# Unread matmuls ahead of the first rows and at the first norm's broadcast, rows loaded ahead of weights, and the sample's first states loaded ahead of stores

## The chip, the cores and the metric

The kernel runs on one core of one Trainium2 chip. The metric is the device time of one execution in microseconds, the median of several runs. The engines are TensorE (PE; its weight loads are listed as PEld), VectorE (DVE), ScalarE (ACT), GpSimd (POOL) and SyncE (SP), which here only issues DMAs.

## The reference

One step of a decoder layer is computed for 1024 prompt rows and 32 sample rows (8 batches of 4), width 1024, in float32:

```python
def hybrid_layer(x, lp, ssd_conv_prev, ssm_prev, ffn_conv_prev, kv_buf):
    hn = rmsnorm(x, lp['norm1'])
    z, xbc, dt_raw, q, k, v = jnp.split(hn @ lp['w_in'], SPLITS, axis=-1)
    y_ssd, ssd_conv_new, ssm_new = ssd_mixer(z, xbc, dt_raw, ssd_conv_prev, ssm_prev, lp)
    ...   # q and k are normed; the window of attention is 128
    x = x + jnp.concatenate([y_ssd, y_att], axis=-1) @ lp['w_out']
    hn = rmsnorm(x, lp['norm2'])
    u, ffn_conv_new = causal_dwconv(hn @ lp['w_up'], ffn_conv_prev, lp['ffn_conv_w'], lp['ffn_conv_b'])
    gate, val = jnp.split(u, 2, axis=-1)
    x = x + (jax.nn.silu(gate) * val) @ lp['w_down']
    return x, (ssm_new, ssd_conv_new, k_new, v_new, ffn_conv_new)
```

The SSD mixer convolves x, B and C over four rows, scans chunks of 128 rows with a carried state for 8 heads, multiplies by silu(z) and norms. For the sample the scan starts from given states (`h0`); for the prompt from zero. All new states are outputs.

## The kernel before

The 1056 rows of prompt and sample are the columns of `xT`; the width of 1024 is eight tiles of 128 partitions, `x[0]` to `x[7]`. Products in float32 are done as three matmuls: each operand is split into a high part (`xh`, `uh`, by ScalarE) and a low part (`xl`, `ul`, by VectorE), and high by high, high by low and low by high are added up. `dense` (L147) does this over three column parts of 352, `token_major` (L199) with rows of 128 tokens.

**Start.** `ones` is a 128x128 tile of ones (L207). For each k the rows `x[k]` are loaded (L222; k = 0 in three parts) and split, their squares are summed into `ssum`, and for even k 256 columns of the two first weights `w01` are loaded (L115). All loads are issued by SP, in the order of the code. The norm is applied late: the matmuls run on rows that are not yet normed, `stats` (L155) sums the squares over partitions with `ones`, VectorE computes `rstd` (L134 to L140), and `bcast` transposes it with the identity (L170) and ScalarE copies it to `rstd_bc` (L171), by which `conv_in` multiplies the matmuls' results (L261). Ahead of `bcast` stands the first `token_major` product, `kv0`.

**Middle.** A string `PLAN` lists units of work: SSD chunks (u), z blocks, splits, output pieces (o). In `ssd_unit` the state step is a matmul into `st` (L660) followed by VectorE's `sn` (L668). For the sample the unit loads the states of the past in four pairs (`h0`, in two buffers; L682), multiplies with them (L685), and stores the rows of this step to `smps` (L678, L679).

**Second norm and FFN.** The rows are held in halves of 528 columns (tp = 0, 1) as `acc`. `out_piece(m, q)` adds the output projection (L778). `half_prep(tp)` calls `half_rstd(tp)`, which sums squares (L852), computes `v` on VectorE (L854, then L134 to L140), transposes it (L859) and copies it (ACT, L861); then eight products by the norm (L871) and the splits into `x2h` (ACT L883) and `x2l` (DVE L884, with differences L888) follow. The up projection is seven products per pair of tiles and half (`product`, L990), its operands made from the weights by L923, L925, L935 and L936, its results combined by L998, L1004, L1010, L1012 and others. Then come the convolution, the gate and the down projection (L1105).

A scheduler of the framework orders each engine's instructions by its own timeline, so that the order on an engine is not that of the code, and an edit early in the program can move rows much later.

Of the kernel before, what the change touches and what calls it, by code (L numbers as in the profile page):

```python
# [9 lines left out]
F32 = mybir.dt.float32  # L10
F32R = mybir.dt.float32r
I32 = mybir.dt.int32
AF = mybir.ActivationFunctionType
# [5 lines left out]
T = 1056  # L19
NP = 1024  # L20
NS = 32
NB = 8
NPAIR = 22
EPS = 1e-6
NEG = -1e30
PC = 352
# [20 lines left out]
def kernel(ctx, tc, xT, wxbc, wkv, wq, wz, wout, wup, wdn, cols, rows, cst, idm,  # L47
# [61 lines left out]
    def unit():  # L109
        return (wr.tile([128, 1024], F32, tag="raw", name="raw"), wp.tile([128, 1024], F32R, tag="uh", name="uh"),  # L110
                wp.tile([128, 1024], F32R, tag="ul", name="ul"))

    def load_part(u, src, a, b, e=None):
        raw, hi, lo = (t[:, a:b] for t in u)
        sp.dma_start(out=raw, in_=src)  # L115
        act.activation(out=hi, in_=raw, func=AF.Copy)  # L116
        n = (b - a) // (1 if e else 1)
        for i in range(0, b - a, n):
            (e or dve).tensor_tensor(out=lo[:, i:i + n], in0=raw[:, i:i + n], in1=hi[:, i:i + n].bitcast(F32),  # L119
                                     op=ALU.subtract)  # L120
# [41 lines left out]

    def bcast(pp):

        for a, n in ((0, 512), (512, 512), (NP, NS)):
            ps = bank(pp)
            for o in range(0, n, 128):
                m = min(n, 128)
                t = (a + o) // 128
                pe.transpose(out=ps[:, o:o + m], in_=b3(rstd[:m, t:t + 1], m, 128), identity=ident[:m, :m])  # L170
            act.activation(out=rstd_bc[:, a:a + n], in_=ps[:, :n], func=AF.Copy)  # L171
# [33 lines left out]


    dve.memset(ones, 1.0)  # L207
    act.activation(out=rstd[:, 0:1], in_=ones[:, 0:1], func=AF.Exp)
    x = [None] * 8
    with tc.tile_pool(name="st", bufs=1, side="right", reuse_waits="tile") as stp:  # L210
        ssum = stp.tile([128, T], F32, name="ssum")
        w01 = [unit(), unit()]
        for k in range(8):
            if k % 2 == 0:
                for m in range(2):
                    load_part(w01[m], wxbc[m][:, 128 * k:128 * k + 256], 128 * k, 128 * k + 256)
            if k == 0:
                sp.dma_start(out=colt, in_=cols)
            xr = yp.tile([128, T], F32, tag="y", name="xr")
            x[k] = x_pair(xp)  # L220
            for a, b in ([(0, PC), (PC, 2 * PC), (2 * PC, T)] if k == 0 else [(0, T)]):
                sp.dma_start(out=xr[:, a:b], in_=xT[k][:, a:b])  # L222
                split(xr[:, a:b], x[k], col(C_N1 + k), a, b)
            if k == 0:
                act.activation(out=ssum, in_=xr, func=AF.Square)
            else:
                sq = stp.tile([128, T], F32, tag="sq", name="sq", bufs=2)
                act.activation(out=sq, in_=xr, func=AF.Square)
                dve.tensor_tensor(out=ssum, in0=ssum, in1=sq, op=ALU.add)
        w01 = [u[1:] for u in w01]  # L230
        sp.dma_start(out=idt, in_=idm)
        wkvu = [load_unit(wkv[:, 3 * i:min(8, 3 * i + 3), :].rearrange("p k c -> p (k c)"), 264 * min(3, 8 - 3 * i))
                for i in range(3)]
        sp.dma_start(out=sstt, in_=sst)
        sp.dma_start(out=rowt, in_=rows)
        sp.dma_start(out=cs, in_=cst[:, 0:K_LOW])
        dve.tensor_scalar(out=chalf, in0=colt[:, C_CW:C_CW + 40], scalar1=0.5, scalar2=None, op0=ALU.mult)
        two = pc.tile([128, 2, 512], F32, tag="sc", name="two")
        ps01 = [[bank(pm) for _ in range(3)], [two[:, 0], two[:, 1], bank(pq)]]
        for k in range(8):  # L240
            for m in range(2):
                for p in range(3):
                    dense(ps01[m][p][:, :PC], wl(w01[m]), xr_(x, p), [k], first=k == 0, last=k == 7)
                if k == 7 and m == 0:
                    stats(stp, ssum, pq)
        kv0 = token_major(264, wkvu, 3, 0, bank(pq))
        bcast(pq)
# [350 lines left out]
    def ssd_unit(g, t, p, carry, te):  # L598
# [5 lines left out]
        hs = slice(4 * g, 4 * g + 4)  # L604
        px = psd.tile([128, 512], F32, tag="px", name="px", bufs=2)
        if smp:
            f4 = p.tile([128, 512], F32, tag="Cs", name="f4", bufs=2)[:, 0:384].rearrange("p (i c t) -> p i c t", i=3, c=4)
            for i, f in enumerate((x0, x1, Bm)):
                pool.tensor_copy(out=f4[:, i], in_=b3(f[:, tok].unsqueeze(1), 128, 4, NS))
# [65 lines left out]
                      rhs=xw[:m, 64 * h:64 * h + 64], start=True, stop=True)  # L675
        cm = p.tile([128, 8, NS], F32, tag="cm", name="cm", bufs=1)
        pool.tensor_tensor(out=cm, in0=b3(Cm[:, NP:T].unsqueeze(1), 128, 8, NS), in1=bmask, op=ALU.mult)
        sp.dma_start(out=smps[g, :, 0:128], in_=bt)  # L678
        sp.dma_start(out=smps[g, :, 128:384], in_=xd)  # L679
        for j in range(4):  # L680
            h0 = p.tile([128, 2, 256], F32, tag="h0", name="h0", bufs=2)
            sp.dma_start(out=h0, in_=h0T[:, g, 2 * j:2 * j + 2])  # L682
            for b in range(2):
                r = slice(32 * (2 * j % 4 + b), 32 * (2 * j % 4 + b) + 32)
                pe.matmul(out=yy[r, 256:512], lhsT=cm[:, 2 * j + b], rhs=h0[:, b], start=j < 2, stop=j >= 2)  # L685
        y = p.tile([128, 256], F32, tag="xd0", name="ys")
        dve.tensor_tensor(out=h4(y), in0=h4(yy[:, 256:512]),
                          in1=b3(te[:, 8 + 4 * g:12 + 4 * g].unsqueeze(2), 128, 4, 64), op=ALU.mult)
# [160 lines left out]
    def half_rstd(tp):  # L849
        ps = bank()  # L850
        for j in range(6):
            pe.matmul(out=ps[:88, j:j + 1], lhsT=ssum[tp][:, 88 * j:88 * j + 88], rhs=ones[:, 0:1], start=True, stop=True)  # L852
        v = pt_.tile([128, 2, 6], F32, tag="v2", name="v2")
        dve.tensor_scalar(out=v[:88, 0], in0=ps[:88, 0:6], scalar1=1.0 / D, scalar2=EPS, op0=ALU.mult, op1=ALU.add)  # L854
        rsqrt(pt_, v[:88, 1], v[:88, 0], 88, 6)
        for q in range(2):
            ps = bank()
            for j in range(3):
                pe.transpose(out=ps[:, 88 * j:88 * j + 88], in_=b3(v[:88, 1, 3 * q + j:3 * q + j + 1], 88, 128),  # L859
                             identity=ident[:88, :88])  # L860
            act.activation(out=ssum[tp][:, q * QC:q * QC + QC], in_=ps[:, :QC], func=AF.Copy)  # L861
        return ssum[tp]

    X2 = [{}, {}]

    def half_prep(tp):

        rb = half_rstd(tp)
        for m in (4, 5, 6, 7, 0, 1, 2, 3):
            h = half(m, tp)  # L870
            dve.scalar_tensor_tensor(out=h, in0=h, scalar=col(C_N2 + m), in1=rb, op0=ALU.mult, op1=ALU.mult)  # L871
# [73 lines left out]
    for i, m in enumerate((4, 5, 6, 7, 0, 1, 2, 3)):  # L945
        if i >= 4:
            w[m] = None
        for q in (2, 3):
            out_piece(m, q)
            if i == 0 and q == 2:  # L950
                half_prep(0)
        half_done(m, 1, i == 0)
    up_load(0)
    for j in range(7):
# [93 lines left out]
    for n, (cp, groups) in enumerate(SETS):  # L1048
        for g in groups:
# [15 lines left out]
                conv(cp, 0)  # L1065
            last = (n, *g), done
            if g == (0, 0):
                half_prep(1)
    product(*last[0], 6)
    conv(last[0][1], 1)  # L1070
    sp.dma_start(out=fco, in_=fcot)
# [188 lines left out]
```

## Time and profile before

| | us |
|---|---|
| median of three runs | 1192.26 |
| the three runs | 1192.59, 1192.26, 1187.1 |
| the profiled execution | 1191.26 |
| its span | 1189.5 |
| TensorE busy in it | 1149.4 (97%) |
| VectorE busy in it | 906.0 (76%) |
| ScalarE busy in it | 513.0 (43%) |

The mean granted clock of TensorE over the span is 0.990. The profile shows one execution; an engine's share is a mean over stages, so that each stage has to be looked at by itself. In rows of the profile an engine is followed by the line of the kernel, the operation and `output<-inputs`; text in brackets is the idle time ahead and what ended it.

### The profile page before, as it was taken

What the parts mean: (1) busy time and instruction counts of PE and PEld (TensorE: products, weight loads), DVE (VectorE), ACT (ScalarE), POOL (GpSimd) and SP (SyncE); (2) the same over time, 40 slices, a digit from 0 to 9 for tenths busy, and PEclk for the clock granted to TensorE, in tenths of its full rate; (3) what the DMA queues carried; (4) which work ended last, traced back from release to release, by engine and by line L of the source; (5) the groups of instructions that cost most, each with busy time, mean ns of one, the idle gap of its engine ahead of it and who ended that gap; (6) DMA issues with size and microseconds to landing.
All of it is one profiled execution on the core that took longest, in us unless ns stands there. A gap on an engine that the chain in (4) does not pass through costs nothing.

```text
span 1189.5 us, 22050 instructions
## 1 busy us (share of the span) xinstructions
PE 1149.4 (97%) x8614; PEld 1106.5 (93%) x8614; DVE 906.0 (76%) x1886; ACT 513.0 (43%) x1048; POOL 134.8 (11%) x300
## 2 busy tenths in 40 slices
PE   8899989999979999899999999999999999999998
PEld 7899878888957999789999999999999999999998
DVE  7678868666888578998777777787777877677764
ACT  7435553446774334555455454545454421112110
POOL 0000001022253000011011010101010011001000
PEclk9999989998999999899999999999999999999999
DMA  8111102113465523122222222222222944224203
GB/s 295 63 60 62 33 19 75 48 50 111 131 221 160 173 73 131 36 81 98 74 72 90 73 90 73 90 73 81 81 71 75 380 149 160 97 91 133 92 9 147
DMA packets 52360, 122.52 MB, mean 103 GB/s; under 512 B 9232, under 2 KB 19984, under 8 KB 52240
## 3 DMA queue, kind: packets, MB, share of 16 engines
q1 hardware_dynamic: 52256, 121.12, 29.8%
q8 instruction: 67, 1.10, 0.4%
q14 instruction: 37, 0.30, 0.1%
HBM read 94.86 MB, written 27.26 MB: 103 GB/s over the span
## 4 chain that ended last, share of the span: by engine, by line
PE 89%; DVE 7%; DMA 2%; ACT 1%; issue 1%; SPq 0%; POOL 0%; DVEq 0%; ACTq 0%
PE ps L147 40%; PE ps L990 35%; PE ps L199 7%; PE sc L503 1%; PE ps L525 1%; DVE x2l L884 1%; DVE au L936 1%; DVE c L1032 1%; PE two L147 1%; DMA raw<-in_wup 1%; PE ps L517 1%; PE yy L653 1%; PE st L660 1%; PE ps L339 0%; PE px L611 0%
## 5 line engine op out<-in xcount | busy, mean ns | idle before, releaser
L990 PE MATMUL ps<-x2h,au 128*128 128x264 f32 x2464 | 456.1, 286 | 8.5 <-DVE au L936 2.8
L990 PEld LDWEIGHTS ps<-x2h,au 128*128 128x128 f32 x2464 | 385.0, 189 | 10.6 <-DVE au L936 3.5
L990 PE MATMUL ps<-x2l,au 128*128 128x264 f32 x1232 | 349.4, 285 | 0.1
L990 PEld LDWEIGHTS ps<-x2l,au 128*128 128x128 f32 x1232 | 232.8, 189 | 0.3 <-DVE x2l L884 0.3
L1105 DVE TENSOR_TENSOR acc<-acc,ps 128x352 f32<-128x352 f32 x264 | 131.5, 517 | 66.0 <-PE ps L147 65.5
L147 PE MATMUL ps<-xh,uh 128*128 128x264 f32 (+3 forms) x528 | 163.3, 315 | 8.9 <-ACT xh L182 5.9
L147 PE MATMUL ps<-gh,ul 128*128 128x352 f32 x528 | 170.1, 322 | 0.0
L147 PE MATMUL ps<-gl,uh 128*128 128x352 f32 x528 | 170.0, 322 | 0.0
L147 PE MATMUL ps<-gh,uh 128*128 128x352 f32 x528 | 167.8, 322 | 0.0
L147 PE MATMUL ps<-xh,ul 128*128 128x264 f32 (+3 forms) x528 | 163.7, 311 | 0.0
L147 PE MATMUL ps<-xl,uh 128*128 128x264 f32 (+3 forms) x528 | 163.3, 310 | 0.3 <-POOL xl L180 0.3
L116 ACT ACTIVATE uh<-raw 128x1024 fp32r<-128x1024 f32 (+3 forms) x59 | 55.9, 953 | 188.0 <-PE ps L147 166.9
L1032 DVE SCALAR_TENSOR_TENSOR c<-u,colt,c 128x1072 f32<-128x1072 f32 x88 | 116.7, 1329 | 3.6 <-ACT c L1030 3.6
L147 PEld LDWEIGHTS ps<-xh,uh 128*128 128x128 f32 x528 | 99.7, 190 | 13.7 <-ACT xh L182 6.3
L147 PEld LDWEIGHTS ps<-xl,uh 128*128 128x128 f32 x528 | 100.6, 191 | 1.8 <-POOL xl L180 0.9
L147 PEld LDWEIGHTS ps<-xh,ul 128*128 128x128 f32 x528 | 100.6, 190 | 1.0 <-issue 0.3
L936 DVE TENSOR_TENSOR au<-raw,au 128x512 fp32r<-128x512 f32 x115 | 78.8, 690 | 27.3 <-ACT au L935 27.3
L147 PEld LDWEIGHTS ps<-gl,uh 128*128 128x128 f32 x528 | 99.2, 188 | 0.4
L147 PEld LDWEIGHTS ps<-gh,ul 128*128 128x128 f32 x528 | 99.3, 188 | 0.0
L147 PEld LDWEIGHTS ps<-gh,uh 128*128 128x128 f32 x528 | 98.8, 188 | 0.0
L935 ACT ACTIVATE au<-raw 128x512 fp32r<-128x512 f32 x115 | 71.0, 625 | 60.7 <-DVE raw L923 31.5
L119 DVE TENSOR_TENSOR ul<-raw,uh 128x1024 fp32r<-128x1024 f32 (+3 forms) x55 | 60.5, 1105 | 7.0 <-ACT uh L116 6.9
(290 smaller groups left out, 1768.4 us busy)
## 6 DMA issues: line engine op xcount, KB each, us to landing
raw<-in_wup SPq DMA_DIRECT2D x46, 512.0 KB, 3.5
gr<-gd SPq DMA_DIRECT2D x22, 528.0 KB, 5.3
gd<-c SPq DMA_DIRECT2D x22, 512.0 KB, 2.6
raw<-in_wdn SPq DMA_DIRECT2D x22, 512.0 KB, 3.8
raw<-in_wout SPq DMA_DIRECT2D x12, 512.0 KB, 3.4
acc<-in_xT SPq DMA_DIRECT2D x16, 264.0 KB, 5.0
accd<-acc SPq DMA_DIRECT2D x16, 264.0 KB, 2.5
acc<-accd SPq DMA_DIRECT2D x8, 528.0 KB, 8.4
```

Of the source, the lines that this page charges most:

```text
L116: act.activation(out=hi, in_=raw, func=AF.Copy)
L119: (e or dve).tensor_tensor(out=lo[:, i:i + n], in0=raw[:, i:i + n], in1=hi[:, i:i + n].bitcast(F32), op=ALU.subtract)
L147: pe.matmul(out=ps, lhsT=w(a, k), rhs=x(b, k), start=first and k == ks[0] and i == 0, stop=last and k == ks[-1] and i == 2)
L199: pe.matmul(out=ps[:m, :n], lhsT=x[k][c][:, a:a + m], rhs=w[k // nk][b][:, o:o + n], start=k == 0 and i == 0, stop=k == 7 and i == 2)
L503: pe.matmul(out=sb[:, v, c].rearrange("p i k -> p (i k)"), lhsT=qT[a][r, c], rhs=kT[b][r, o:o + 256], start=i == 0, stop=i == 2)
L517: pe.transpose(out=pt[:, h], in_=P[:, h], identity=ident)
L525: pe.matmul(out=po[64 * v:64 * v + 64, 0:256].rearrange("p (c q) -> p c q", c=2), lhsT=(vall[:, t - i] if i or not t else vdif[:, t - 1])[ ...
L935: act.activation(out=u[:, 0:512], in_=src, func=AF.Copy)
L936: dve.tensor_tensor(out=u[:, 512:1024], in0=src, in1=u[:, 0:512].bitcast(F32), op=ALU.subtract)
L990: pe.matmul(out=ps, lhsT=wgt[:, 512 * a + 128 * k:512 * a + 128 * k + 128], rhs=xx[b][:, k], start=opens and k == 0 and i == 0, stop=k == ...
L1032: dve.scalar_tensor_tensor(out=c[:, 0:n], in0=u[:, j:j + n], scalar=col(C_FW + 3 * m + j), in1=c[:, 0:n], op0=ALU.mult, op1=ALU.add)
L1105: dve.tensor_tensor(out=o, in0=o, in1=ps[:, :PC], op=ALU.add)
```

## The change

It has five parts.

1. Ahead of everything else on TensorE stand nine matmuls of `ones` by `ones` (`NWARM`), whose result nobody reads.
2. The first 352 columns of `x[0]` are the first load on SP, then the constants `colt`; the first two weight parts are issued on ScalarE's queue, ahead of its first activation, which brings the table load. For k = 2, 4, 6 nothing moves between queues.
3. `bcast` begins with ten unread matmuls of `ones` into a bank of its own.
4. In the sample's SSD unit the first two pairs of states are loaded at the start of the unit, and the stores to `smps` stand behind the loop over the states.
5. `half_prep` is cut in two: for the first half the sum of squares and `v` come after the output piece (4, 2) as before, and the transposes and the rest after the piece (4, 3). For the second half both stay together.

```diff
+NWARM = 9
...
     def load_part(u, src, a, b, e=None):
         raw, hi, lo = (t[:, a:b] for t in u)
-        sp.dma_start(out=raw, in_=src)
+        if src is not None:
+            sp.dma_start(out=raw, in_=src)
...
     def bcast(pp):
 
+        hold = bank(pp)
+        for i in range(10):
+            pe.matmul(out=hold[:, 0:128], lhsT=ones, rhs=ones, start=True, stop=True)
...
     dve.memset(ones, 1.0)
-    act.activation(out=rstd[:, 0:1], in_=ones[:, 0:1], func=AF.Exp)
     x = [None] * 8
+
+    idle = bank(pq)
+    for i in range(NWARM):
+        pe.matmul(out=idle[:, 0:128], lhsT=ones, rhs=ones, start=True, stop=True)
     with tc.tile_pool(name="st", bufs=1, side="right", reuse_waits="tile") as stp:
         ssum = stp.tile([128, T], F32, name="ssum")
         w01 = [unit(), unit()]
+        for m in range(2):
+            act.dma_start(out=w01[m][0][:, 0:256], in_=wxbc[m][:, 0:256])
+        act.activation(out=rstd[:, 0:1], in_=ones[:, 0:1], func=AF.Exp)
         for k in range(8):
-            if k % 2 == 0:
+            xr = yp.tile([128, T], F32, tag="y", name="xr")
+            x[k] = x_pair(xp)
+            if k == 0:
+                sp.dma_start(out=xr[:, 0:PC], in_=xT[k][:, 0:PC])
+                sp.dma_start(out=colt, in_=cols)
+                for m in range(2):
+                    load_part(w01[m], None, 0, 256)
+            elif k % 2 == 0:
                 for m in range(2):
                     load_part(w01[m], wxbc[m][:, 128 * k:128 * k + 256], 128 * k, 128 * k + 256)
-            if k == 0:
-                sp.dma_start(out=colt, in_=cols)
-            xr = yp.tile([128, T], F32, tag="y", name="xr")
-            x[k] = x_pair(xp)
             for a, b in ([(0, PC), (PC, 2 * PC), (2 * PC, T)] if k == 0 else [(0, T)]):
-                sp.dma_start(out=xr[:, a:b], in_=xT[k][:, a:b])
+                if k or a:
+                    sp.dma_start(out=xr[:, a:b], in_=xT[k][:, a:b])
                 split(xr[:, a:b], x[k], col(C_N1 + k), a, b)
...
         if smp:
+
+            h0s = []
+            for j in range(2):
+                h0s.append(p.tile([128, 2, 256], F32, tag="h0", name="h0", bufs=2))
+                sp.dma_start(out=h0s[j], in_=h0T[:, g, 2 * j:2 * j + 2])
...
-        sp.dma_start(out=smps[g, :, 0:128], in_=bt)
-        sp.dma_start(out=smps[g, :, 128:384], in_=xd)
         for j in range(4):
-            h0 = p.tile([128, 2, 256], F32, tag="h0", name="h0", bufs=2)
-            sp.dma_start(out=h0, in_=h0T[:, g, 2 * j:2 * j + 2])
+            if j < 2:
+                h0 = h0s[j]
+            else:
+                h0 = p.tile([128, 2, 256], F32, tag="h0", name="h0", bufs=2)
+                sp.dma_start(out=h0, in_=h0T[:, g, 2 * j:2 * j + 2])
...
+        sp.dma_start(out=smps[g, :, 0:128], in_=bt)
+        sp.dma_start(out=smps[g, :, 128:384], in_=xd)
...
+        return v
+
+    def half_bcast(tp, v):
...
-    def half_prep(tp):
-
-        rb = half_rstd(tp)
+    def half_prep(tp, v):
+
+        rb = half_bcast(tp, v)
...
             if i == 0 and q == 2:
-                half_prep(0)
+                v0 = half_rstd(0)
+            elif i == 0:
+                half_prep(0, v0)
...
             if g == (0, 0):
-                half_prep(1)
+                half_prep(1, half_rstd(1))
```

Lines move with the edit: L147 becomes L149, L170 becomes L175, L199 becomes L204, L682 becomes L626 (first two pairs) and L703, L774 becomes L797, L871 becomes L897, L884 becomes L910, L936 becomes L962, L998 becomes L1026 and L1012 becomes L1040.

Three places show what this makes of the engines' orders. The first is TensorE at the broadcast. Before, the last rows of `kv0` (L199) are followed by the transposes of `rstd` (L170):

```order
L199 MATMUL ps<-uh,xh 128x264
L199 MATMUL ps<-uh,xl 128x264
L199 MATMUL ps<-ul,xh 128x264
L170 MATMUL ps<-idt,rstd 128x128 x8
L170 MATMUL ps<-idt,rstd 128x32
```

After, at the same place, with L204 for `kv0`, L169 for the unread matmuls and L175 for the transposes:

```order
L204 MATMUL ps<-ul,xh 128x264
L169 MATMUL ps<-ones 128x128 x4
L204 MATMUL ps<-uh,xh 128x264
L204 MATMUL ps<-uh,xl 128x264
L169 MATMUL ps<-ones 128x128 x2
L204 MATMUL ps<-ul,xh 128x264
L204 MATMUL ps<-uh,xh 128x264
L204 MATMUL ps<-uh,xl 128x264
L204 MATMUL ps<-ul,xh 128x264
L169 MATMUL ps<-ones 128x128 x4
L175 MATMUL ps<-idt,rstd 128x128 x8
L175 MATMUL ps<-idt,rstd 128x32
```

The ten unread matmuls stand among the last six of `kv0`, four of them right ahead of the transposes.

The second place is SP's queue at group 0's second pair and group 1's first pair of states (`h`). Before:

```order
L774 DMA acc<-in_xT 128x528
L628 DMA ab<-acd 128x512
L682 DMA h_3937<-in_h0T 128x512
L682 DMA h_3941<-in_h0T 128x512
L774 DMA acc<-in_xT 128x528 x3
L115 DMA raw<-in_wout 128x1024
L682 DMA h_4631<-in_h0T 128x512
L682 DMA h_4635<-in_h0T 128x512
```

After:

```order
L797 DMA acc<-in_xT 128x528
L648 DMA ab<-acd 128x512
L703 DMA h_3956<-in_h0T 128x512
L703 DMA h_3960<-in_h0T 128x512
L797 DMA acc<-in_xT 128x528 x3
L117 DMA raw<-in_wout 128x1024
L626 DMA h_4615<-in_h0T 128x512
L626 DMA h_4617<-in_h0T 128x512
```

Both pairs stand where they stood; only the lines that issue them differ.

The third place is VectorE ahead of the second half's norm: L871 (after: L897) are the eight products by the norm, L998 (L1026) a result of the up projection, L936 (L962) the low part of an operand, L884 (L910) the split of the normed rows, and `v` the norm's last step. Before:

```order
L140 SCALAR_TENSOR_TENSOR v_5791<-rs 88x6
L936 TENSOR_TENSOR au<-raw,au 128x512
L1012 TENSOR_TENSOR u<-u,ps 128x264
L936 TENSOR_TENSOR au<-raw,au 128x512 x2
L871 SCALAR_TENSOR_TENSOR acc<-acc,colt,ssum_5198 128x528 x8
L998 TENSOR_TENSOR u<-s_5934,ps 128x264
L998 TENSOR_TENSOR u<-s_5907,ps 128x264
L884 TENSOR_TENSOR x2l<-acc,x2h 128x528
L936 TENSOR_TENSOR au<-raw,au 128x512
L925 TENSOR_TENSOR t_6025<-raw 128x512
L884 TENSOR_TENSOR x2l<-acc,x2h 128x528 x5
```

After:

```order
L962 TENSOR_TENSOR au<-raw,au 128x512
L1040 TENSOR_TENSOR u<-u,ps 128x264
L962 TENSOR_TENSOR au<-raw,au 128x512
L140 TENSOR_TENSOR rs<-rs 88x6
L962 TENSOR_TENSOR au<-raw,au 128x512
L141 TENSOR_TENSOR rs<-rs 88x6
L142 SCALAR_TENSOR_TENSOR v_5812<-rs 88x6
L1026 TENSOR_TENSOR u<-s_5955,ps 128x264
L1026 TENSOR_TENSOR u<-s_5928,ps 128x264
L962 TENSOR_TENSOR au<-raw,au 128x512
L897 SCALAR_TENSOR_TENSOR acc<-acc,colt,ssum_5219 128x528 x8
L951 TENSOR_TENSOR t_6046<-raw 128x512
```

The two L1026 and one L962 stand ahead of the eight products by the norm, where L998 and L936 stood behind them. On TensorE 156 of the first half's products (L990) stand ahead of the second half's transposes, where 134 stood.

## The prediction

> **What bounds the kernel now.** I read the page first, then a table of stretches, then what TensorE waited for, and last the timeline and the chain of waits at the places that the change touches.
>
> ```profile
> PE 1149.4 (97%) x8614; PEld 1106.5 (93%) x8614; DVE 906.0 (76%) x1886; ACT 513.0 (43%) x1048; POOL 134.8 (11%) x300
> PE 89%; DVE 7%; DMA 2%; ACT 1%; issue 1%; SPq 0%; POOL 0%; DVEq 0%; ACTq 0%
> ```
>
> TensorE is busy 97% of the span and carries 89% of the chain that ended last. Next, stretches: span, busy time of PE, PEld, DVE, ACT and POOL, granted clock, DMA share and GB/s.
>
> ```profile
> 41.60:45.00 3.40, 3.37 (x17) 3.37 (x18) 2.90 (x8) 1.75 (x3) 0.66 (x4) 0.57 0.19 74
> 270.00:280.00 10.00, 8.72 (x37) 8.14 (x36) 6.43 (x13) 7.86 (x23) 3.03 (x5) 0.66 0.40 128
> 484.00:500.00 16.00, 12.63 (x76) 11.78 (x75) 15.94 (x27) 7.84 (x15) 0.00 (x0) 0.79 0.17 65
> 500.00:535.00 35.00, 30.90 (x244) 29.77 (x242) 33.32 (x53) 21.13 (x34) 4.78 (x12) 1.00 0.20 67
> 535.00:929.00 394.00, 393.33 (x3228) 393.12 (x3228) 299.62 (x482) 194.39 (x348) 47.71 (x153) 1.00 0.25 84
> 929.00:1185.00 256.00, 255.54 (x1599) 255.16 (x1600) 190.21 (x325) 46.16 (x48) 18.70 (x20) 1.00 0.37 134
> ```
>
> From 535 us to the end TensorE is full at clock 1.00: 650 of 1189.5 us in which an edit that leaves the matmuls alone can move nothing. The row of 535 to 929 also prices a matmul of the products: 394.00/3228 = 0.12 us. What is left is the idle time and the half-speed stretches ahead of 535 us. The waits of TensorE (total us, times, longest) name the largest:
>
> ```profile
> PE ps L147 <- ACT xh L182: 5.9, 2, 5.7
> PE st L660 <- DVE sn L668: 3.3, 3, 1.5
> PE ps L170 <- issue: 2.9, 1, 2.9
> PE ps L990 <- ACT x2h L883: 2.4, 1, 2.4
> PE yy L685 <- DMA h<-in_h0T: 2.4, 1, 2.4
> ```
>
> Four of the five lie at places that the change edits or moves (the first matmul, the broadcast, the second norm, the sample's states), and none is over 6 us: the stake is a few us. Differences under 0.5%, 6 us, can hardly be told from no change on this kernel.
>
> **The start: unread matmuls, rows ahead of weights.** Columns: start, duration, engine, line, operation.
>
> ```profile
> 0.83 0.17 DVE L207 MEMSET ones<- 128x128 f32 x1 [0.83 <-PEq L1235]
> 2.12 1.85 SPq L222 DMA_DIRECT2D xr<-in_xT  x4
> 5.68 0.66 PE L147 MATMUL ps<-xh,uh 128*128 128x352 f32 x1 [5.68 <-ACT xh L182]
> 6.72 0.50 PE L147 MATMUL ps<-xl,uh 128*128 128x352 f32 x1
> 7.01 0.50 PE L147 MATMUL ps<-xh,ul 128*128 128x352 f32 x1
> ...
> 11.38 0.32 PE L147 MATMUL ps<-xh,ul 128*128 128x352 f32 x1
> ...
> 13.70 1.31 DVE L183 SCALAR_TENSOR_TENSOR xl<-xr,colt,xh 128x1056 fp32r<-128x1056 f32 x1
> 15.24 0.32 PE L147 MATMUL ps<-xl,uh 128*128 128x352 f32 x1
> ```
>
> The chain of waits over the same time (start, us, what) says which transfer holds TensorE:
>
> ```profile
> 3.07 4.87 DMA xr<-in_xT
> ...
> 8.60 1.54 PE ps L147 x4
> ...
> 12.35 1.12 PE ps L147 x7
> ```
>
> The matmuls follow each other at 7.01 − 6.72 = 0.29 us until 11.38, and at 1.12/7 = 0.16 us after it: the first 5.7 us run at half speed. What is done ahead of 8.60 is worth nothing faster, since the third part of x[0] (issued 3.07, landed 7.94) holds TensorE there. From 8.60 to 11.38 stand about ten matmuls; at full speed they would save 10 × 0.13 = 1.3 us. But TensorE then runs into its feed: the low half of x[2] is ready at 13.70 + 1.31 = 15.01 and is first read at 15.24, a slack of 0.23 us. More is had only if the rows themselves come earlier. The change issues the first two weight parts on ScalarE's queue, so that the row parts come off SP up to two issue slots (1.85/4 = 0.46 each) earlier, 0.9 us; the bytes are the same, so the landings gain between 0 and 0.9, and I take 0.5, the middle. The start is worth −0.2 to −1.2 us; taken −0.7. ScalarE's own table load and first activation go behind its two issues; its first product is wanted only when a weight has landed, which covers them.
>
> The nine unread matmuls need only `ones`, ready at 1.00. The trace has none of their shape; the nearest is the statistics row in the next fence, where an FP32 matmul shows as two records: 1.83/18 = 0.1 us a record, 0.2 a matmul at full speed and 0.4 at half. Nine are 3.6 us, over at about 4.7, ahead of the first matmul at 5.68. They delay nothing unless the rows come a whole microsecond earlier.
>
> The Trainium skill ("TensorE: Matmul & The Clock Gate", Part 1) says that the clock is released after one busy window of about 3.4 us, and that the windows run freely and don't start with the kernel. By that rule 3.6 us of unread matmuls fill a window only by luck, and a miss puts the release one window later; no run here shows it yet. By it the release at 11.38 would come one or two windows earlier, at 8.0 or 4.6, both ahead of 8.60, so the sum would be the same by either and 1.3 us poorer only if no window at all were gained.
>
> **The first norm's broadcast.** First the chain of waits, then the timeline.
>
> ```profile
> 31.92 1.83 PE ps L155 x18
> 33.75 3.15 PE ps L199 x24
> 36.90 2.86 issue
> ```
>
> ```profile
> 38.15 1.23 DVE L119 TENSOR_TENSOR ul<-raw,uh 128x1024 fp32r<-128x1024 f32 x1 [1.15 <-ACT uh L116]
> 39.49 0.17 DVE L140 SCALAR_TENSOR_TENSOR rstd<-rs 128x9 f32<-128x9 f32 x1
> ...
> 42.33 0.42 PE L199 MATMUL ps<-uh,xl 128*128 128x264 f32 x1
> 42.55 0.42 PE L199 MATMUL ps<-ul,xh 128*128 128x264 f32 x1
> ```
>
> TensorE stands idle for 2.86 us until VectorE has finished `rstd`, whose last two steps stand behind the split of a weight (38.15). The unread matmuls don't shorten that, since the transposes read `rstd`. What they can change is what follows: from 42.1 to 45.4 the matmuls are 42.55 − 42.33 = 0.22 us apart instead of 3.15/24 = 0.13, the stretch at 0.57 in the table. Some 16 matmuls lose 0.09 us each, 1.5 us. Ten unread matmuls are 10 × 0.2 = 2.0 us, over at 36.90 + 2.0 = 38.9, ahead of `rstd` at 39.66: they hold nothing up, and leave 0.8 us of the gap. Six of them delay the last token-major rows, whose readers want `rstd` too. The term is 0 to −1.6; taken −1.5, since the gap that stays is a third of the one before the slow stretch.
>
> **The sample's first states.** Their loads and the stores of `smps` lie on SP. In SP's order each group's first pair stands where it stood, with group 0's ahead of the stores already, and the stores move by a row or two. The 2.4 us wait of L685 is for group 0's second pair, which stays behind the same rows:
>
> ```profile
> 334.36 0.90 SPq L682 DMA_DIRECT2D h<-in_h0T  x2
> 339.68 0.63 PE L685 MATMUL yy<-h,cm 128*32 128x256 f32 x4 [2.38 <-DMA h<-in_h0T]
> ```
>
> It is issued at 334.36 and awaited until 339.68. The edit is worth 0, with ±0.5 for a slot on the queue.
>
> **What the order does beside it.** From about 160 us on the order differs on every engine. Between the state steps of the SSD (the L660 matmuls) stand 288 dense matmuls instead of 270: 18 × 0.12 = 2.2 us of work that can lie where TensorE waits, the 3.3 us for `sn` among it. I take half, −1.2, with 0 and −2.3 as bounds, for not every one falls into a gap. Other reordered waits I price at ±3, about the second entry of the table of waits, and at 0 in the sum.
>
> **The second norm.** Here the change does harm, I think.
>
> ```profile
> 465.32 0.43 DVE L778 TENSOR_TENSOR acc<-acc,ps 128x264 f32<-128x264 f32 x1 [1.91 <-PE ps L147]
> ...
> 483.90 5.52 DVE L871 SCALAR_TENSOR_TENSOR acc<-acc,colt,ssum 128x528 f32<-128x528 f32 x8 [0.39 <-ACT ssum L861]
> 489.34 0.76 DVE L998 TENSOR_TENSOR u<-s,ps 128x264 f32<-128x264 f32 x2
> 490.64 0.68 DVE L936 TENSOR_TENSOR au<-raw,au 128x512 fp32r<-128x512 f32 x1
> ```
>
> The first half's norm comes one output piece later. VectorE sat idle for 1.91 us just before 465.3, where the products begin, so that half stays hidden. The second half is the bottleneck: from 484 to 500 VectorE is busy 15.94 of 16 us, and TensorE idles 3.4. In the new order the two L998 and the L936 that stood behind the eight L871 stand ahead of them, and 156 of the first half's products, not 134, stand ahead of the transposes: 22 × 0.12 = 2.6 us. The L871 start up to 2.6 us later, and 0.76 + 0.68 = 1.4 us of VectorE's work has come forward for it. The saturated stretch ends between 2.6 − 1.4 = 1.2 and 2.3 us later (with only part of that work moved); taken +1.5, nearer the first, since all three of these rows have changed sides.
>
> **Sum.** −0.7 − 1.5 + 0 − 1.2 + 1.5 = −1.9. The profiled execution took 1191.26 us (span 1189.5), 1.0 below the median of the runs, 1192.26: 1191.26 − 1.9 = 1189.4.
>
> **The rivals.** *All of it comes.* The half-speed start costs half of 11.38 − 5.68, 2.85 us, and earlier rows feed a faster TensorE; the dip goes (−1.6), the gaps are filled (−2.3), the second norm doesn't slip: −6.8, 1184.5. For it: each part acts on a stretch of its own. Against it: the 0.23 us of slack at x[2], and the order ahead of the L871.
>
> That page of the Trainium skill prices a throttled stretch at half its time; the start of this rival agrees with it.
>
> *The change doesn't do what it says.* The clock stays low at both places, the rows land as before, and refill and slip cancel: 1191.3, up to 1192.8 with the slip of 1.5. For it: 0.8 us of the gap stays, and the rows' bytes share the same DMA engines.
>
> *Slower.* The reordered waits put TensorE at half speed more often. The stretch from 270 to 280 at 0.66 lost 0.34 × 10 = 3.4 us of full speed, 484 to 500 at 0.79 as much. Two more such stretches are +6.8, the second norm +2.3, less 2.2 for start and broadcast: +6.9, 1198.2. It decides from the second new stretch on. Against it: the wait up to 339.68 was 2.38 us, and the SSD is filled better, not worse.
>
> **How the numbers follow.** The sum has 0.60, with ±3 for the order, 1186.4 to 1192.4; all of it 0.20; no effect 0.11; slower 0.09. Faster by over 0.5% is under 1186.3 against the median: the second case and the low edge of the first, 0.23. Slower is above 1198.2: the last case, 0.09, with as much of it below as other mishaps lie above. Within is the rest, 0.68. The range reaches into the second case and to 1.2 below the last: 1183.5 to 1197.
>
> **What would show it.** Right: matmuls of 0.32 us from 8.6 on; none of 0.42 behind the first transposes; the L685 wait unchanged; TensorE idle over 4 us in the stretch of the second half's norm. Wrong: rows that land over 1 us earlier, half-speed stretches between 160 and 480 that weren't there, or a second norm that holds TensorE no longer than 3.4 us.

## The result, and the profile after

The change makes the kernel slower: 1203.18 us median of five runs, against 1191.3 of the kernel before; ratio 1.0097, 95% interval 1.0078 to 1.0115. The forecast was 1189.4 with a range up to 1197.0, so both sign and range missed.

The cores' lines (span, mean granted clock of TensorE), before and then after, the latter with the busy times of the engines and the shares of the chain:

```profile
core 0: 1189.5 us, clock 0.990
```

```profile
core 0: 1201.5 us, clock 0.979
PE 1166.8 (97%) x8652; PEld 1119.5 (93%) x8652; DVE 916.8 (76%) x1886; ACT 518.1 (43%) x1048; POOL 140.5 (12%) x300
PE 89%; DVE 6%; ACT 2%; DMA 2%; issue 1%; POOL 0%; SPq 0%; ACTq 0%; DVEq 0%
```

The span grew by 12.0 us. TensorE's idle time did not: span less busy time was 1189.5 − 1149.4 = 40.1 us and is 1201.5 − 1166.8 = 34.7. Its busy time grew by 17.4 with 38 more records, the nineteen unread matmuls. The clock goes with it: 0.990 of 1189.5 us leaves out 11.9 us of full speed, 0.979 of 1201.5 leaves out 25.2, which is 13.3 more. (The clock's records begin 11.3 and 6.6 us after the first instruction; what lies ahead of them is counted as full speed here.)

To find the place, the span is cut where the same instruction stands in both: first and last state step of the SSD (L660, after L680), first product of the up projection (L990, after L1018). Columns as in the table of stretches of the prediction; before, then after:

```profile
271.90:363.80 91.90, 83.38 (x650) 73.26 (x651) 72.08 (x183) 64.67 (x187) 30.34 (x45) 0.97 0.43 140
363.80:465.10 101.30, 98.96 (x811) 95.23 (x810) 74.40 (x175) 37.76 (x66) 11.99 (x21) 1.00 0.42 137
465.10:540.00 74.90, 67.18 (x514) 65.00 (x513) 68.23 (x124) 39.95 (x74) 6.76 (x18) 0.95 0.24 81
```

```profile
271.30:373.00 101.70, 95.27 (x695) 81.44 (x696) 77.93 (x202) 66.21 (x193) 32.67 (x47) 0.89 0.40 129
373.00:473.40 100.40, 97.98 (x766) 94.58 (x766) 67.45 (x153) 35.45 (x59) 11.07 (x16) 0.95 0.43 138
473.40:552.00 78.60, 68.47 (x519) 65.36 (x518) 68.96 (x126) 41.53 (x75) 6.86 (x20) 0.96 0.22 77
```

Up to 271 us the kernel after is 0.6 us ahead. The SSD takes 101.7 us instead of 91.9, but holds 45 records more, which came in from the next stretch (766 instead of 811 there). The two stretches together hold the same 1461 records and take 8.9 us more, 202.1 instead of 193.2. TensorE is idle for less in them (8.9 us against 10.9), and the clock fell from 0.97 to 0.89 and from 1.00 to 0.95. The second norm's stretch takes 3.7 us more for five more products. Behind it nothing changed.

Inside the SSD, ten microseconds at a time, before and after:

```profile
340.00:350.00 10.00, 6.60 (x61) 4.59 (x58) 7.86 (x20) 5.66 (x16) 5.50 (x8) 1.00 0.60 217
350.00:360.00 10.00, 7.55 (x69) 6.13 (x68) 8.81 (x29) 9.27 (x30) 2.56 (x4) 1.00 0.34 110
```

```profile
340.00:350.00 10.00, 7.94 (x45) 4.62 (x43) 5.61 (x16) 2.55 (x6) 3.98 (x6) 0.60 0.52 185
350.00:360.00 10.00, 9.28 (x56) 7.34 (x57) 9.50 (x31) 8.05 (x25) 3.92 (x5) 0.66 0.22 73
380.00:390.00 10.00, 10.00 (x62) 7.97 (x62) 6.64 (x15) 4.32 (x10) 7.90 (x9) 0.73 0.96 311
400.00:410.00 10.00, 8.60 (x58) 8.07 (x57) 6.01 (x21) 2.89 (x4) 0.00 (x0) 0.83 0.48 138
```

This is the trap of the column of busy time: from 340 to 350 TensorE is "busier" than before (7.94 against 6.60 us) and yet does less, 45 records instead of 61. The two orders don't hold the same records there, but at half speed each lasts longer. Granted clock and the count in brackets have to be read beside it. The records of the clock put half speed at 337.7 (for 10.2 us), 351.3 (6.8), 378.6 (6.8) and 402.5 (3.4): 27.3 us that the profiled execution before did not have. That execution is the exception, though. In seven of the runs below TensorE's records between the first and last state step are the same as before and in the same order, and their traces have 10.2 to 17.1 us of half speed between 330 and 410. Against these the profiled execution after has 10 to 17 us more, not 27.

What stands ahead of the first of them (timeline after, TensorE and VectorE):

```profile
339.32 0.90 PE L631 MATMUL px<-idt,fm 128*128 128x128 f32 x3 [3.06 <-DVE cb L660]
```

```profile
335.84 1.49 DVE L185 TENSOR_TENSOR xl<-fm,xh 128x384 fp32r<-128x384 f32 x2
337.25 1.21 DVE L121 TENSOR_TENSOR ul<-raw,uh 128x1024 fp32r<-128x1024 f32 x1
338.38 0.68 DVE L652 TENSOR_TENSOR Cs<-Cs,fm 128x512 f32<-128x512 f32 x1
338.99 0.28 DVE L660 TENSOR_TENSOR cb<-px,cs 128x128 f32<-128x128 f32 x1
```

TensorE waits 3.06 us for a VectorE row of 0.28 us that frees a bank (`px`) and in this order stands behind 3.15 us of other rows (335.84 to 338.99), most of them splits. At about the same place it waited 2.38 us before, for another thing.

The start and the broadcast, in the chain of waits after:

```profile
30.01 1.83 PE ps L157 x18
31.84 2.40 PE ps L204 x18
34.23 0.89 PE ps L169 x8
...
36.30 0.91 PE ps L169 x8
37.21 1.04 issue
38.24 0.64 PE ps L175 x4
```

and, as a stretch, what follows them:

```profile
40.70:44.10 3.40, 3.40 (x18) 3.40 (x17) 2.91 (x7) 1.29 (x1) 0.66 (x4) 0.50 0.03 11
```

The statistics begin at 30.01 instead of 31.92, the transposes at 38.24 instead of 39.76. The ten unread matmuls fill all but 1.04 us of the wait, and in this execution the half-speed stretch comes all the same.

### The profile page after: what moved, and what is told of

The parts are those of the page before. It is cut to its first block, busy times and chain, and to the rows that moved or that the text cites. A ratio compares the mean times of both kernels' runs of the same rounds, so it can differ in the third digit from the quotient of the medians.

```text
span 1201.5 us, 22177 instructions
## 1 busy us (share of the span) xinstructions
PE 1166.8 (97%) x8652; PEld 1119.5 (93%) x8652; DVE 916.8 (76%) x1886; ACT 518.1 (43%) x1048; POOL 140.5 (12%) x300
## 4 chain that ended last, share of the span: by engine, by line
PE 89%; DVE 6%; ACT 2%; DMA 2%; issue 1%; POOL 0%; SPq 0%; ACTq 0%; DVEq 0%
PE ps L149 38%; PE ps L1018 34%; PE ps L204 7%; PE sc L518 1%; PE ps L540 1%; DMA raw<-in_wup 1%; PE yy L673 1%; PE st L680 1%; DVE x2l L910 1%; PE yy L675 1%; DVE au L962 1%; PE ps L532 1%; PE px L631 1%; PE two L149 1%; DMA raw<-in_wout 0%
## 5 line engine op out<-in xcount | busy, mean ns | idle before, releaser
L1018 PE MATMUL ps<-x2h,au 128*128 128x264 f32 x2464 | 455.9, 286 | 8.1 <-ACT x2h L909 5.2
L1018 PEld LDWEIGHTS ps<-x2h,au 128*128 128x128 f32 x2464 | 384.4, 189 | 10.1 <-ACT x2h L909 5.7
L1018 PE MATMUL ps<-x2l,au 128*128 128x264 f32 x1232 | 349.0, 285 | 2.0 <-DVE x2l L910 1.9
L1018 PEld LDWEIGHTS ps<-x2l,au 128*128 128x128 f32 x1232 | 232.6, 189 | 2.9 <-DVE x2l L910 2.9
L149 PE MATMUL ps<-gh,ul 128*128 128x352 f32 x528 | 170.1, 322 | 0.0
L149 PE MATMUL ps<-gl,uh 128*128 128x352 f32 x528 | 170.0, 322 | 0.0
L149 PE MATMUL ps<-gh,uh 128*128 128x352 f32 x528 | 167.9, 322 | 0.6 <-ACT gh L184 0.6
L149 PE MATMUL ps<-xh,uh 128*128 128x264 f32 (+3 forms) x528 | 163.4, 315 | 2.8 <-ACT uh L118 1.2
L149 PE MATMUL ps<-xl,uh 128*128 128x264 f32 (+3 forms) x528 | 164.8, 313 | 0.9 <-POOL xl L185 0.6
L149 PE MATMUL ps<-xh,ul 128*128 128x264 f32 (+3 forms) x528 | 162.8, 310 | 0.2 <-DVE ul L121 0.2
L149 PEld LDWEIGHTS ps<-xh,uh 128*128 128x128 f32 x528 | 100.7, 192 | 6.7 <-DVE u L276 1.5
L149 PEld LDWEIGHTS ps<-xl,uh 128*128 128x128 f32 x528 | 101.1, 192 | 4.0 <-POOL xl L185 1.6
L149 PEld LDWEIGHTS ps<-xh,ul 128*128 128x128 f32 x528 | 100.7, 191 | 1.1 <-DVE ul L121 0.5
L149 PEld LDWEIGHTS ps<-gh,uh 128*128 128x128 f32 x528 | 98.8, 188 | 0.9 <-ACT gh L184 0.9
L149 PEld LDWEIGHTS ps<-gl,uh 128*128 128x128 f32 x528 | 99.2, 188 | 0.4
L149 PEld LDWEIGHTS ps<-gh,ul 128*128 128x128 f32 x528 | 99.3, 188 | 0.0
L962 DVE TENSOR_TENSOR au<-raw,au 128x512 fp32r<-128x512 f32 x115 | 78.8, 690 | 24.0 <-ACT au L961 23.4
```

The costliest lines, as they stand in the source:

```text
L149: pe.matmul(out=ps, lhsT=w(a, k), rhs=x(b, k), start=first and k == ks[0] and i == 0, stop=last and k == ks[-1] and i == 2)
L962: dve.tensor_tensor(out=u[:, 512:1024], in0=src, in1=u[:, 0:512].bitcast(F32), op=ALU.subtract)
L1018: pe.matmul(out=ps, lhsT=wgt[:, 512 * a + 128 * k:512 * a + 128 * k + 128], rhs=xx[b][:, k], start=opens and k == 0 and i == 0, stop=k == ...
```

## The experiments

Two theories stood against each other. Theory A: the broadcast's unread matmuls lead the scheduler to another order of the SSD, whose waits put TensorE at half speed. Theory B: the moved loads and stores, or the cut of `half_prep`, cost the time. The orders alone sort the parts of the change: without the ten unread matmuls TensorE's order in the SSD is that of before (270 dense matmuls between the state steps), with them it has 288 or, without the start's parts, 273.

**The whole change without the broadcast's unread matmuls.**

```diff
     def bcast(pp):
-        hold = bank(pp)
-        for i in range(10):
-            pe.matmul(out=hold[:, 0:128], lhsT=ones, rhs=ones, start=True, stop=True)
```

> The whole change without the ten unread matmuls of the broadcast. TensorE's order in the SSD is then nearly that of before (270 dense matmuls between the state steps, at the same places). Theory A (these ten matmuls move the order of the SSD, whose new waits put TensorE at half speed four times more between 337 and 406 us): no half-speed stretch there, 9 to 11 us less than the changed kernel, 1191 to 1195, of which +3 is the second norm. Theory B (the moved loads and stores, at the start or of the sample's states, cause it): still slower than before by 8 or more, 1199 to 1204.

Measured: 1188.62, ratio to before 0.9987 (0.9971 to 1.0003). The loss is gone with these three lines. It is 2.4 us below theory A's own lower bound. The expectation of no half-speed stretch there fell: the profiled execution, the fastest of the twelve, has 6.8 us from 333.8 and 3.4 from 381.6.

```profile
330.00:340.00 10.00, 6.05 (x35) 3.65 (x35) 7.16 (x16) 6.33 (x19) 5.70 (x8) 0.69 0.68 227
```

So these matmuls are the cause of the loss, but some half speed in the SSD belongs to the old order as well.

**These matmuls alone.** The three lines above, added to the kernel before.

> Before, with the ten unread matmuls of the broadcast alone. TensorE's order in the SSD differs from before and also from the changed kernel (273 dense matmuls between the state steps). Theory A: half-speed stretches appear between 330 and 410 us, +4 to +12, 1195 to 1203. Theory B: as before, 1188 to 1192, perhaps 1.5 less if the slow stretch behind the broadcast goes.

Measured: 1196.38, ratio 1.0045 (1.0024 to 1.0065). As theory A had it, 2.0 us of work in a wait cost 5.6, with half-speed stretches at 344.9, 385.8 and 399.5:

```profile
340.00:350.00 10.00, 7.83 (x58) 5.95 (x55) 9.37 (x26) 5.35 (x15) 4.84 (x7) 0.83 0.59 202
380.00:390.00 10.00, 8.11 (x51) 7.38 (x51) 7.66 (x28) 3.07 (x6) 0.87 (x2) 0.83 0.57 195
```

Half speed doesn't explain the 5.6 us, though. These stretches add up to 10.2 us, as many as in the run above. Over all its executions span times (1 − clock), the full speed that was lost, is 15.3 us in the mean, and 14.5 in the 25 executions of the kernel before that ran beside it. Most of what this order costs lies elsewhere, and where was not found.

**The start alone**: parts 1 and 2 of the change, nothing else.

> Before, with the nine unread matmuls at the start and the rows ahead of the weights, and nothing else. The order from 46 us on is nearly that of before. Both theories: half speed only until about 7 us; the first norm's wait begins 1.5 to 2 us earlier than 36.9. If the wait for rstd shifts with it, 1189 to 1190; if rstd is held by the load of a later weight, half of that. Theory B differs only if the loads disturb what follows: 1195 or more.

Measured: 1187.45, ratio 0.9973 (0.9958 to 0.9988): 3.2 us faster than before, more than was expected, and the only part that was run alone whose interval lies wholly below 1. Its chain at the broadcast:

```profile
31.51 1.83 PE ps L157 x18
...
36.49 1.71 issue
38.20 0.64 PE ps L172 x4
```

The transposes come 1.56 us earlier; the rest of the gain lies within the interval.

**The whole change without the cut of `half_prep`.**

```diff
-                v0 = half_rstd(0)
-            elif i == 0:
-                half_prep(0, v0)
+                half_prep(0, half_rstd(0))
```

> The whole change without the cut of half_prep for the first half. The SSD's order is word for word that of the changed kernel, so theory A: the half-speed stretches between 337 and 406 us stay, and the time falls only by what the second norm lost, 2 to 4 us: 1199 to 1201. Were the cut the cause of most of the loss, 1192 to 1194.

Measured: 1201.51, ratio 1.0091 (1.0065 to 1.0117). The cut is not the cause of most of the loss. The half-speed stretches stayed in part: the profiled execution, the fastest of four, has 10.2 us from 335.6 and 3.4 from 376.5, half of the 27.3, and TensorE waits 3.64 us for `v` ahead of the first half's transposes, which it doesn't in the changed kernel.

**Fourteen unread matmuls in the broadcast instead of ten**, in the whole change:

```diff
-        for i in range(10):
+        for i in range(14):
```

> The whole change with fourteen unread matmuls in the broadcast instead of ten. With fourteen, TensorE's order in the SSD is nearly that of before again (270 dense matmuls between the state steps, at the same places). Order theory (the count matters only through the order that the scheduler then chooses): 10 to 14 us less than the changed kernel, 1187 to 1191, no 10 us stretch at half speed near 340. Rival (unread matmuls at the broadcast cost by themselves, or by the bank that they hold): as slow or slower, 1202 to 1205.

Measured: 1191.74, ratio 1.0016 (1.0001 to 1.0032). Four more unread matmuls, 0.8 us of added work, make the changed kernel 11.4 us faster by the medians and 9.6 by the ratios. The rival that the matmuls or their bank cost the 12 us by themselves is out. A smaller cost is not: with TensorE's order in the SSD the same, this version is 3.5 us slower by the ratios than the one without them (0.9987; the two intervals nearly touch), and the next run is 2.5 us slower than the start alone. In this run's chain their 28 records take 0.89 + 0.44 + 1.78 = 3.1 us. The expectation of no 10 us stretch at half speed near 340 fell: the profiled execution has one, from 335.6. The order of before has half speed there too, but less in all: 10.2 us between 330 and 410 against 27.3.

**The start with fourteen**, without the states and the cut: the start alone plus the broadcast's lines with 14.

> Before, with the start's parts and fourteen unread matmuls in the broadcast; no moved states and no cut of half_prep. Its order in the SSD is nearly that of before. Order theory: as the start alone (1187.5), or up to 1.5 less where the slow stretch behind the broadcast goes: 1185.5 to 1188. Rival: the unread matmuls cost by themselves: 1190 or more.

Measured: 1188.9, ratio 0.9994 (0.9978 to 1.001). Beside the start alone (1187.45) it gains nothing. The chain shows why:

```profile
30.53 1.83 PE ps L157 x18
32.36 3.52 PE ps L204 x18
...
38.35 1.78 PE ps L169 x16
40.14 0.45 PE ps L175 x4
```

```profile
33.20:36.60 3.40, 3.40 (x18) 3.40 (x17) 2.12 (x9) 1.11 (x2) 0.00 (x0) 0.50 0.68 240
```

There is no wait left at the broadcast: TensorE itself is the last now, and the transposes come at 40.14, 1.94 us later than in the start alone. Half speed comes earlier, from 33.2, right behind the statistics (L157), eighteen records of one column each. The window of 3.41 us ahead of it is busy throughout, with 1.99 us of these records and 1.42 of others:

```profile
29.80:33.20 3.40, 3.40 (x30) 3.37 (x29) 1.68 (x7) 0.61 (x2) 0.43 (x4) 1.00 0.54 130
```

The unread matmuls didn't move it there. Of the fourteen traces (before, after and the twelve runs) six have half speed at this place, and two of the six hold no matmul in the broadcast: the whole change without them (from 33.4) and the rows alone (from 33.6). In all six the clock's raster puts all eighteen records into one window. In the other eight no window holds more than 1.93 us of them, beside 1.49 of other records, and half speed doesn't follow. So these records, busy in the trace, seem to count for little with the clock.

**One unread matmul instead of ten**, in the whole change (`range(1)`).

> The whole change with one unread matmul in the broadcast instead of ten. It takes 0.2 us of TensorE, but the scheduler's order in the SSD differs from before and from the changed kernel alike. Order theory: the time is that of another order, not that of one matmul less or more: 1193 to 1204, with half-speed stretches between 330 and 410. Rival (the work of the unread matmuls counts): as without them, 1187 to 1190.

Measured: 1194.46, ratio 1.0038 (1.002 to 1.0057). One matmul of 0.2 us, and the kernel is some 6 us slower than with none (ratio 0.9987): again the order's price. Its profiled execution, the fastest of ten with a span of 1189.4, has half-speed stretches of 3.4 us at 333.4 and 394.8.

**A filled gap.** The changed kernel with ten more unread matmuls at the place of the 3.06 us wait, inside the output piece (2, 0). They share a bank with that piece's sums and spoil them, so that `y` isn't the reference's there.

```diff
+            dense(ps, wl(w[m]), rhs, range(4), last=False)
+            for i in range(10):
+                pe.matmul(out=pb[:, 384:512], lhsT=ones, rhs=ones, start=True, stop=True, ...)
+            dense(ps, wl(w[m]), rhs, range(4, 8), first=False)
```

> The changed kernel, with ten more unread matmuls (2.0 us) in the output piece (2, 0), at the row behind which TensorE waited 3.06 us at 336.3; the order up to that row is word for word that of the changed kernel, behind it some dense matmuls move. Clock theory (the loss is half speed that follows this wait): the stretch of 10.24 us at half speed from 337.7 does not come, 3 to 6 us less than the changed kernel, 1197 to 1200. Rival (the loss is the waits themselves, and the clock only goes along): 1203 to 1206.

Measured: 1197.3, 5.9 us less than the changed kernel by the medians and 3.8 by the ratios (1.0065, interval 1.0042 to 1.0088), with 2.0 us more work. Timeline and stretches:

```profile
334.11 2.40 PE L804 MATMUL ps<-ones 128*128 128x128 f32 x20
337.99 0.55 PE L631 MATMUL px<-idt,fm 128*128 128x128 f32 x3 [1.00 <-DVE cb L660]
```

```profile
330.00:340.00 10.00, 8.87 (x69) 6.63 (x68) 8.92 (x11) 9.21 (x26) 5.30 (x6) 1.00 0.94 286
340.00:350.00 10.00, 7.18 (x53) 5.26 (x52) 9.79 (x25) 5.72 (x17) 5.63 (x7) 0.83 0.51 161
350.00:360.00 10.00, 10.00 (x86) 8.29 (x86) 7.20 (x28) 6.74 (x22) 2.42 (x4) 1.00 0.29 97
```

The wait of the same row fell to 1.00 and the stretches of 10.2 and 6.8 us to one of 3.4. Over the executions the mean clock is 0.986 instead of 0.980. The order behind the gap differs somewhat, so this supports the clock as the cause and doesn't prove it by itself.

**The start with a filled gap.** The start alone, with ten unread matmuls at that place (after three of the eight parts of the piece, with `start=False`, which leaves the sums as they are).

> Before with the start's parts alone, and ten unread matmuls (2.0 us) inside the output piece (2, 0), shortly ahead of the wait of some 2.2 us near 336 us; the order is otherwise that of the run with the start alone. Clock theory: the half-speed stretch that began at 336.2 in that run does not come, 1184 to 1187. Rival (the unread matmuls only push what stands behind them): 1188 to 1190.

Measured: 1187.37, ratio 0.9979 (0.9963 to 0.9995): the same as the start alone. In the profiled execution, the slowest of the twelve, half speed did not come at 336, but it came elsewhere:

```profile
366.00:376.00 10.00, 10.00 (x46) 8.48 (x46) 4.64 (x13) 1.88 (x4) 4.74 (x7) 0.50 0.48 154
```

Filling this one gap gained nothing.

**The cut of `half_prep` alone.**

> Before with the cut of half_prep for the first half alone; all rows up to the second norm are those of before. From the traces of the changed kernel (the stretch from the first product on about 3 us longer): slower by 1 to 3.5 us. By the prediction's own term: slower by 1.2 to 2.3. If the second norm isn't held by it: no difference.

Measured: 1193.77, ratio 1.0025 (1.0008 to 1.0042): 3.0 us slower, between 1.0 and 5.0. In its profiled execution, one at the median, the stretch that the cut changes, from the first product of the up projection to the first sum of the down projection, takes 473.4 us instead of 471.7. The rest of the difference lies ahead, where TensorE's order is that of before: half speed for 17.1 us in the SSD, from 336.6, 350.2 and 387.8.

```profile
350.00:360.00 10.00, 9.98 (x65) 8.90 (x62) 7.70 (x26) 7.84 (x28) 1.72 (x2) 0.66 0.22 67
```

**The nine unread matmuls alone, and the rows ahead of the weights alone.**

> Before with the nine unread matmuls at the start alone; rows and weights are loaded as before. The third part of x[0] then holds TensorE at about 8.6 as before, so that full speed gains at most 1.3 us, and 0.2 if the low half of x[2] ends last: 0 to 1.3 us faster. Rival (the start's gain is all clock): 2.5 to 3.3 us faster.

> Before with the rows loaded ahead of the weights alone, and no unread matmul. The rows land about 1 us earlier; TensorE stays at half speed until about 10. Feed theory (rows bring the larger part): 1 to 2 us faster. Rival (without the clock the rows bring nothing, since the half-speed matmuls of x[0] and x[1] are then the slower part): 0 to 0.5 us faster.

Measured: 1190.58, ratio 0.9991 (0.9974 to 1.0009), and 1190.99, ratio 1.0002 (0.9988 to 1.0015). Neither is different from before, while both together are 3.2 us faster. The chain at the broadcast, of the matmuls alone and then of the rows alone:

```profile
31.07 1.83 PE ps L156 x18
...
36.05 2.18 issue
38.23 2.29 PE ps L171 x9
```

```profile
30.65 1.83 PE ps L157 x18
...
37.08 1.73 issue
38.81 0.64 PE ps L172 x4
```

In these two executions, both the slowest of their twelve, each brings the transposes forward, by 1.5 and 1.0 us; the medians don't confirm it. What follows took it back: from the first state step to the up projection they take 196.4 and 196.9 us instead of 193.2, with the same records and more half speed. The expectation that one of them would carry the gain fell.

## Why the prediction was wrong

**The step that failed** is the one on the order: −1.2 for dense matmuls that fill idle time, and "Other reordered waits I price at ±3, … and at 0 in the sum." In place of −1.2 ± 3 the SSD and the stretch behind it took 8.9 us more for the same 1461 records. The count of dense matmuls between the state steps (288 instead of 270) was read right, and idle time did fall, by 2.0 us, but the clock lost more. What happened is the rival *Slower*, given 0.09: more half-speed stretches, which it let decide from the second new one on. Its argument against itself was wrong: that a wait of 2.38 us before 339.68 did no harm. In all seven runs with TensorE's SSD order of before, half speed came between 333 and 339 us; in the start alone it stands behind a wait of 2.22 us for the same states:

```profile
336.00:343.00 7.00, 5.09 (x28) 3.21 (x26) 4.44 (x12) 2.56 (x6) 4.49 (x7) 0.51 0.44 161
```

One profiled execution without the stretch was no evidence that the place is safe.

That the order sets the time is shown: with the old order of TensorE's records the time from the first state step to the up projection was 191.6 to 196.9 us in eight traces, with that of the changed kernel 202.1, and 203.8 without the cut of `half_prep`. How much of that is the clock is less sure. Over five executions of the changed kernel span times (1 − clock) is 24.0 us in the mean, over 101 of the kernel before 13.6, while the mean span grew by 11.8; so some 10.4 of these at most are the clock's. From one execution of the kernel before to another a us of lost clock goes with only 0.6 us of span; by that, an estimate, the clock accounts for 6 to 7 us, and the rest stays open.

**The broadcast**, −1.5, gained no time, although its mechanism held in most traces. Half speed begins behind the broadcast, between 38 and 43 us, in six of the seven traces without these matmuls, and in one of six with ten or fourteen of them, the profiled one (0.50 from 40.7 to 44.1; TensorE was busy for 2.03 of the 3.40 us ahead of it, so that closing two thirds of the gap was not enough there). Three of the other five have it behind the statistics instead. What the term left out is the order that these matmuls lead to, and with fourteen their own work.

**The start**, −0.7 with −1.2 as its end, was too small: alone it measured −3.2 (−1.4 to −5.0). Why is not shown. The feed looks mis-sized if the two first traces are compared, before and then after, since the low half of x[1] begins 1.8 us earlier where 0.5 was taken:

```profile
10.62 1.32 DVE L183 SCALAR_TENSOR_TENSOR xl<-xr,colt,xh 128x1056 fp32r<-128x1056 f32 x1 [1.46 <-ACT xh L182]
```

```profile
8.79 1.32 DVE L188 SCALAR_TENSOR_TENSOR xl<-xr,colt,xh 128x1056 fp32r<-128x1056 f32 x1 [1.76 <-ACT xh L187]
```

But these are the two ends of a scatter. In ten traces with the rows ahead of the weights this row begins between 8.79 and 10.28 (10.28 in the start alone), in four without between 9.86 and 10.62. The means differ by 0.8 us, within the 0 to 0.9 of the prediction. That full speed began well ahead of 8.6 was right: the clock's records begin 3.9 to 6.6 us after the first instruction in the ten traces with the nine unread matmuls, and 8.9 to 11.3 in the four without.

**The sample's states**, 0: not run alone. The whole change without the broadcast's lines holds them and is not slower than before, so that nothing speaks against 0.

**The second norm**, +1.5, had the right sign and about the right size: the cut alone measured +3.0 (1.0 to 5.0), of which its trace shows 1.7 in the stretch that the cut changes. In the changed kernel that stretch grew by 3.6 (475.3 us). What was missed there is what the L936 (after: L962) that moved ahead of the eight products itself waits for. After:

```profile
495.85 0.63 ACT L961 ACTIVATE au<-raw 128x512 fp32r<-128x512 f32 x1 [0.99 <-DMA raw<-in_wup]
```

```profile
496.52 0.69 DVE L962 TENSOR_TENSOR au<-raw,au 128x512 fp32r<-128x512 f32 x1 [1.84 <-ACT au L961]
497.12 5.52 DVE L897 SCALAR_TENSOR_TENSOR acc<-acc,colt,ssum 128x528 f32<-128x528 f32 x8
```

VectorE stands idle for 1.84 us ahead of its bottleneck, behind a row that waits for ScalarE, which waits for a weight. It was counted by its duration (0.68) and not by what it is behind. This wait belongs to the order and not to the cut: with the cut alone it is 0.43, and with the broadcast's ten matmuls alone, without the cut, 1.72:

```profile
491.78 0.69 DVE L943 TENSOR_TENSOR au<-raw,au 128x512 fp32r<-128x512 f32 x1 [1.72 <-ACT au L942]
```

**The parts don't add up**, and need not: start −3.2, broadcast alone +5.4 and cut +3.0 make 5, the whole measured 11.6 (0.97% of 1191.3). With the start's parts, the broadcast's lines lead to yet another order (288 dense matmuls instead of 273).

## What to carry to other kernels

Where a scheduler sets the order, price the order and not the edit: one, ten or fourteen unread matmuls in a wait gave 1194.5, 1203.2 and 1191.7 us, and only the count moved. Read the granted clock and the count of records beside the busy time, since at half speed an engine looks busier; and count what a moved row is waiting for, not only how long it lasts. The nine unread matmuls at the start left TensorE's order in the SSD as it was, one at the broadcast didn't; the start alone is the version to keep here. And one profiled execution is a sample: of eight with the order of before, only the first had no half speed near 336 us.

## What the runs showed of the hardware

Half speed doesn't follow from idle time alone. All its stretches are 3.4, 6.8 or 10.2 us long (but for the last, which the end of the trace cuts off), on a raster of 3.41 us whose position changes from run to run, and it was seen behind windows in which TensorE's records look busy: with all eighteen one-column matmuls of the statistics (half speed in six traces of six), and in the SSD of the changed kernel behind one that is busy for 2.52 of 3.40 us (half speed from 378.6). How large a share of work keeps the clock up was not settled: before, a window busy for only 1.70 of 3.40 us, from 335.6, was not followed by half speed.

The mean clock goes with most of the spread, too. Over 101 executions of the kernel before, the median span is 1188.8 us and the median clock 0.989, over five of the changed kernel 1201.4 and 0.980; span times clock is 1175.1 us against 1176.3 (medians), and between 1173 and 1180 for every kernel that was run. The highest of these is 1179.4, with the broadcast's ten matmuls alone, where the clock explains little. The Trainium skill ("TensorE: Matmul & The Clock Gate", Part 1) says that the window runs freely, and that the count of slow matmuls at a kernel's start therefore varies from run to run. The traces agree: the first full speed varies by 2.7 us among the ten with the nine unread matmuls and by 2.4 among the four without, less than one window each, and whether half speed follows the statistics varies with the raster as well.
